# A recurrent chain and attention on one core: two buffers of L that stay, PSUM banks handed out in the order asked, and row operations written in larger pieces

## The chip, the cores and the metric

One Trainium2 chip, one of its cores. The metric is the device time of one launch in microseconds (us), the median of three runs. The core has a matrix engine (TensorE, here PE, with its weight loads as PEld), a vector engine (DVE), a scalar engine (ACT), GpSimd (POOL) and a queue that issues the transfers (SP). Each engine works through its own list of instructions in the order in which the program was written; semaphores hold one engine's instruction until another engine has done its part.

## The reference, cut to what matters

A layer of a diffusion backbone over 2048 latent tokens of width 1024 and 256 context tokens, all in fp32: a modulated norm, one input projection, then two groups of heads side by side, an output projection, a second norm and a SwiGLU network. The two groups are what the change is about:

```python
o_na = neighborhood_attention(q, k, v, kc, vc, na_rpb[l])      # 8 heads, 8 x 16 windows + all 256 context keys
o_rw, o_rwc = rwkv_bidir(feat, featc, rw_r_k[l], ...)          # 8 heads, forwards and backwards
mix = jnp.concatenate([o_na, o_rw.astype(h.dtype)], axis=-1) @ w_out[l]
...
def step(s, inp):                                              # the recurrence, token after token
    r_t, w_t, k_t, v_t, a_t, b_t = inp
    sa = jnp.einsum('bhvk,bhk->bhv', s, a_t)
    s = s * w_t[:, :, None, :] + sa[..., None] * b_t[:, :, None, :] + v_t[..., None] * k_t[:, :, None, :]
    return s, jnp.einsum('bhvk,bhk->bhv', s, r_t)
```

The recurrence starts with the 256 context tokens and goes on over the 2048 latent ones, in both directions.

## The kernel before

The program has three stages. `phase1` makes the projections and writes what both groups need to DRAM. `phase2` does the recurrence and the attention together. `phase4` does the output projection and the SwiGLU network. The change touches `phase2` and its planner `emit`, and nothing else.

**The recurrence in `phase2`** is done in blocks of 64 tokens. One *step* s (18 of them, `NS`) covers 128 tokens of each direction, so it has two *chunks* m = 2s and 2s + 1 (36 in all). Four kinds of work make it up:

- `build(s, hp, w)`: for one step and one of four pairs of heads. It loads its part of `d_b` in three transfers, asks for two PSUM banks, multiplies (L1004) and spreads the products into one of 16 units `ga`/`gb` (L1011, L1015 on DVE) and into the tile `lx` (L1010 on ACT). There are 72 of them; two streams, `builds(0)` and `builds(1)`, do two pairs of heads each. Step s uses the units `ga` numbered (4s + hp + 1) mod 16.
- `inverses()`: for each *pair* of steps (2G, 2G + 1; nine of them) the triangular 64x64 blocks in the tile `lx` of the pair are inverted in place. It begins when all eight builds of the pair are done (L1048), transposes on DVE (L1057), eliminates rows on DVE (six pairs of operations at L1070 and L1072, then seven blocks at L1078 to L1083), transposes back (L1087, L1089) and finishes with small matmuls (L1104, L1113) and copies (L1117).
- `lates(g)`: transposed operands of each chunk (L1036, L1039), one bank each.
- `chain(s, c, z, us)`: the recurrence itself, one chunk after the other: a copy of the state (L1175, L1176), matmuls L1185, L1195 and L1205 with a copy between each, two DVE operations that make the new state (L1210, L1225), the output matmuls L1218 and L1222 and their copies (L1230). Step s needs the inverse of its pair (L1151) and its four units.

`lx` holds a pair of steps: its j axis has 8 places, four for the even step and four for the odd one (`j0 = 4 * (s % 2)`). Two such buffers exist, and pair G uses buffer G mod 2. Line 976 makes a build of pair G wait until the chain has done step 2G - 3, the odd step of pair G - 2. Line 978 makes it wait for the step whose unit it takes over, s - 4.

**The attention in `phase2`** has 64 query tiles of 128. `prepare` loads and transposes operands (L670, one bank at a time), `tiles` makes scores (L740), softmax (L775 to L803 on DVE and ACT) and transposes of the probabilities (L790, L793), and `products` multiplies with v (L829) and writes each tile out (L836, L839: one L839 for a tile). Its scores live in four PSUM banks of its own.

**What sets the order.** Each of these is a Python generator that yields what it is about to do. `emit` runs nine of them side by side and writes their instructions down in the order of a plan: `("run", (engine, us))` says how long the next piece holds an engine, `("wait", ...)` and `("post", ...)` tie the streams together, and `("get", z, n)` and `("put", bank)` hand out the two PSUM banks that builds, `lates`, `prepare` and the inverses share. Before, whoever was looked at while enough banks were free got them; one that needs two could be passed by those that need one. What is written between two `run`s stays together. The plan's numbers are only used to choose an order.

Of the kernel before, what the change touches and what calls it, by code (L numbers as in the profile page):

```python
# [11 lines left out]
F32 = mybir.dt.float32  # L12
# [7 lines left out]
P = 128  # L20
# [27 lines left out]
class Run:  # L48
# [5 lines left out]
    def next(s):  # L54
        return s.k.tc.issue_after(s.last) if s.last else nullcontext()
# [806 lines left out]
def emit(banks, *streams):  # L862

    free, when = {}, {}
    banks = [(0.0, b) for b in banks]
    live = [[0.0, i, g, next(g), 0.0] for i, g in enumerate(streams)]
    while live:  # L870
        best, moved = None, False
        for e in list(live):
            while e[3] is not None and e[3][0] != "run":
                op, *args = e[3]
                if op == "post":
                    when[args[0]] = e[0]
                elif op == "put":
                    banks.extend((max(e[0], e[4]), b) for b in args)
                elif op == "get" and len(banks) >= args[1]:
                    banks.sort(key=lambda b: b[0])  # L880
                    for t, b in banks[:args[1]]:
                        e[0] = max(e[0], t)
                        args[0].append(b)
                    del banks[:args[1]]
                elif op == "wait" and all(v in when for v in args):
                    e[0] = max([e[0]] + [when[v] for v in args])
                else:
                    break
                e[3] = next(e[2], None)
                moved = True  # L890
            if e[3] is None:
                live.remove(e)
            elif e[3][0] == "run":
                key = (max(e[0], free.get(e[3][1][0], 0.0)), e[0] + LATE[e[1]], e[1])
                if best is None or key < best[0]:
                    best = (key, e)
        if best is None:
            assert moved or not live, [e[3] for e in live]
            continue
        e = best[1]  # L900
        t0 = e[0]
        for eng, us in e[3][1:]:
            t = max(t0, free.get(eng, 0.0)) if eng != "DMA" else t0
            if eng != "DMA":
                free[eng] = t + abs(us)
            e[4] = t + abs(us) + HOP
            if us > 0:
                e[0] = max(e[0], t + us + HOP)
        e[3] = next(e[2], None)


def phase2(k):
# [4 lines left out]
    with ExitStack() as ctx:  # L917
# [3 lines left out]
        lp = [ctx.enter_context(tc.tile_pool(name=f"lx{i}", bufs=1)) for i in range(2)]  # L921
# [4 lines left out]
        banks = [ps[4 + i].tile([P, 512], F32, name=f"bank{i}") for i in range(2)]  # L926
# [24 lines left out]

            return 128 * s, 128 * (1 - s if s < 2 else 19 - s)

        U, LX, ZV, TT_ = {}, {}, {}, {}

# [7 lines left out]
        def builds(w):  # L965

            for s in range(NS):
                for hp in (w, w + 2):
                    yield from build(s, hp, w)

        def build(s, hp, w):

            G, j0 = s // 2, 4 * (s % 2)
            u = units[(4 * s + hp + SHIFT) % NU]
            if G > 1:
                yield "wait", ("chain", 2 * G - 3)
            if 4 * s + hp >= NU:
                yield "wait", ("chain", (4 * s + hp - NU) // 4)
            if G not in LX:
                LX[G] = lp[G % 2].tile([P, 4, 8, 64], F32, tag="lx", name="lx")  # L980
            lx = LX[G]
            U[s, hp] = u
            src = k.d_b[hp, s]
            for h in range(2):
                if s > 1:
                    nc.sync.dma_start(out=u.ga[H[h], h:3:2 - h], in_=src[H[h], 0:512].rearrange(
                        "p (x j t) -> p x j t", x=2, j=4))
                else:
                    nc.sync.dma_start(out=u.ga[H[h], h], in_=src[H[h], 0:256].rearrange("p (j t) -> p j t", j=4))
            bk = bp.tile([P, 4, 128], F32, tag=f"bk{w}", name="bk", bufs=2)  # L990
            nc.sync.dma_start(out=bk, in_=src[:, 512:1024].rearrange("p (j t) -> p j t", j=4))
            yield "run", ("DMA", 3.0)


            N = 128 if s > 1 else 64
            z = []
            yield "get", z, 2
            yield "run", ("PE", 1.0)
            gp = [v.rearrange("p (j t) -> p j t", j=4) for v in z]
            run = Run(k)  # L1000
            for j in range(4):
                for h in range(2):
                    with run.next():
                        run.last = nc.tensor.matmul(gp[h][:, j, 0:N], bk[H[h], j], u.ga[H[h], h:3:2 - h, j, :] if s > 1  # L1004
                                                    else u.ga[H[h], h, j, :], start=True, stop=True).ins
            dc = "p (d c) t -> p d c t"
            for h in range(2):
                yield "run", ("ACT", -0.45), ("DVE", -0.34)
                ko = H[1 - h]
                nc.scalar.activation(lx[H[h], hp, j0:j0 + 4, :], gp[h][H[h], :, 0:64], AF.Copy)  # L1010
                nc.vector.tensor_tensor(u.ga[ko, h].rearrange(dc, d=2), gp[h][ko, :, 0:64].rearrange(dc, d=2),  # L1011
                                        maskS[ko, :, None, :].to_broadcast([64, 2, 2, 64]), op=ALU.mult)
                if s > 1:
                    yield "run", ("DVE", -0.34)
                    nc.vector.tensor_tensor(u.gb[:, h].rearrange(dc, d=2), gp[h][:, :, 64:128].rearrange(dc, d=2),  # L1015
                                            maskI[:, h, :, None, :].to_broadcast([P, 2, 2, 64]), op=ALU.mult)
                yield "put", z[h]
            yield "post", ("built", s, hp)
# [24 lines left out]
        def inverses():  # L1043
# [2 lines left out]

            for s in range(NS // 2):
                yield ("wait",) + tuple(("built", 2 * s + e, hp) for e in range(2) for hp in range(4))  # L1048
                lx = LX[s]
                lu = lx.rearrange("p g j t -> p (g j) t")  # L1050
                lv = lu[:, :, 0:32]
                for h in range(2):
# [11 lines left out]
                tmp = cp.tile([P, 1024], F32, tag="xT", name="xtmp")  # L1064
                for q in range(1, 4):

                    for i in range(q):
                        yield "run", ("DVE", 0.5)
                        tv = tmp[:, 0:256].rearrange("p (b t) -> p b t", b=8)
                        nc.vector.tensor_tensor(tv, xd[i][q][:, :, None].to_broadcast([P, 8, 32]), x4[:, :, q, :],  # L1070
                                                op=ALU.mult)
                        nc.vector.tensor_tensor(x4[:, :, i, :], x4[:, :, i, :], tv, op=ALU.add)  # L1072
                for q in range(4, 32, 4):

                    m, n = q, 32 - q
                    yield "run", ("DVE", 0.25 + 8 * m * n / 960)
                    tv = tmp[:, :4 * m * n].rearrange("p (c a b) -> p a c b", c=4, a=m)
                    nc.vector.tensor_tensor(tv, x[:, 0:m, q:q + 4, None].to_broadcast([P, m, 4, n]),  # L1078
                                            x[:, None, q:q + 4, q:32].to_broadcast([P, m, 4, n]), op=ALU.mult)
                    half = lambda i, k: tmp[:, i * m * n:(i + k) * m * n]  # L1080
                    nc.vector.tensor_tensor(half(0, 2), half(0, 2), half(2, 2), op=ALU.add)
                    nc.vector.tensor_tensor(half(0, 1), half(0, 1), half(1, 1), op=ALU.add)
                    nc.vector.tensor_tensor(x[:, 0:m, q:32], x[:, 0:m, q:32],  # L1083
                                            half(0, 1).rearrange("p (a b) -> p a b", a=m), op=ALU.add)
# [77 lines left out]
        dq = [(dd, q) for dd in range(2) for q in range(4)]  # L1162

        def chain(s, c, z, us):
            lx, j0 = LX[s // 2], 4 * (s % 2)
            zv = ZV[2 * s + c]
            tt = [TT_.pop((2 * s + c, g)) for g in range(2)]
            zf = z.rearrange("p d q n -> p d (q n)")
# [12 lines left out]
            run = Run(k)  # L1181
# [9 lines left out]
            run = Run(k)  # L1191
# [9 lines left out]
            run = Run(k)  # L1201
# [9 lines left out]
            if s > 1:  # L1211

                yield "run", ("PE", -1.9)
                run = Run(k)
# [23 lines left out]
        def prepare_all():  # L1238
            yield ahead
            yield from prepare  # L1240

        emit(banks, chains(), inverses(), lates(0), lates(1), builds(0), builds(1), at.products(), at.tiles(),
             prepare_all())

# [436 lines left out]
def tile_layer(tc, I):  # L1681
    with ExitStack() as ctx:
        k = K()
        setup(k, ctx, tc, I)
        setup2(k)
        phase1(k)
        with tc.tile_pool(name="mid", bufs=1) as k.mid:
            phase2(k)
            phase4(k)
# [18 lines left out]
```

## Time and profile before

| | us |
|---|---|
| median of three runs | 3523.22 (3523.1 to 3530.65) |
| the profiled execution, its own time | 3522.23 |
| its span | 3520.5 |
| `phase1`, to about | 893 |
| `phase2`, from 893 to about | 1877 |
| `phase4`, from there to the end | 3520.5 |

Over the whole span PE is busy 92% and DVE 68%. In the profile, "span" is the time from the first to the last instruction; a *window* is a stretch of it, in us from its start. For a window the profile gives the time that each engine was busy and, in brackets, the count of its instructions; `PEclk` is the granted share of TensorE's full clock (2.4 GHz), so that 0.75 is a mean over stretches at 2.4 and at 1.2 GHz. A busy PE at a lower clock does less work in the same time.

### The profile page before, as it was taken

The numbers are of one execution on the slowest core, as the hardware profiler recorded it, in microseconds if no ns is written. First come the engines' busy times: TensorE is split into PE (matmuls) and PEld (weight loads), VectorE is DVE, ScalarE is ACT, GpSimd is POOL, SyncE is SP. The second block draws the span as 40 slices with busy tenths as digits, with TensorE's granted clock in tenths as the row PEclk, the third lists the DMA queues.
The fourth block names the chain that finished last, engine by engine and source line by source line (L and its number), as shares of the span: only waits on it lengthen the run. The fifth ranks groups of instructions, "written<-read, shape, count | busy, mean of one in ns | idle before, by whom it ended". The sixth has DMA issues, their size and how long they took to land. (4 is left out here: it accounts for less than half of the span.)

```text
span 3520.5 us, 66352 instructions
## 1 busy us (share of the span) xinstructions
PE 3239.0 (92%) x25202; PEld 2775.8 (79%) x25202; DVE 2396.8 (68%) x4489; ACT 1465.8 (42%) x3186; POOL 1101.2 (31%) x1057
## 2 busy tenths in 40 slices
PE   7899999999879889798856999999899999999999
PEld 5787878789657677576655887888799998899998
DVE  7758786774385766847655754444877778777776
ACT  4524343442445556465433553233333334333332
POOL 3425543453000100100113433333433334433332
PEclk9999999999888899899877999999999999999999
DMA  7546666553634446354326554332422223422222
GB/s 244 160 140 198 189 193 199 160 172 113 194 105 130 142 126 196 97 166 126 87 78 189 183 174 159 96 102 84 150 63 72 67 72 102 135 72 72 66 64 69
DMA packets 461856, 458.50 MB, mean 130 GB/s; under 512 B 56656, under 2 KB 381664, under 8 KB 461536
## 3 DMA queue, kind: packets, MB, share of 16 engines
q1 hardware_dynamic: 461536, 454.25, 42.7%
q8 instruction: 199, 3.26, 0.4%
q14 instruction: 121, 0.99, 0.1%
HBM read 346.37 MB, written 107.75 MB: 129 GB/s over the span
## 5 line engine op out<-in xcount | busy, mean ns | idle before, releaser
L1329 ACT ACTIVATE w<-raw 128x512 fp32r<-128x512 f32 x440 | 270.9, 627 | 497.8 <-PE acc L1618 190.2
L1538 PE MATMUL acc<-ua,w 128*128 128x384 f32 x2464 | 469.8, 336 | 6.0 <-POOL w L1330 2.7
L1618 PE MATMUL acc<-w,fh 128*128 128x512 f32 x1408 | 435.7, 394 | 18.7 <-ACT fh L1329 7.3
L1330 DVE TENSOR_TENSOR w<-raw,w 128x512 fp32r<-128x512 f32 x308 | 273.3, 891 | 247.0 <-ACT w L1329 120.0
L1538 PEld LDWEIGHTS acc<-ua,w 128*128 128x128 f32 x2464 | 433.2, 189 | 9.9 <-POOL w L1330 4.2
L219 PE MATMUL acc<-u,wh 128*128 128x512 f32 (+3 forms) x1120 | 347.9, 390 | 11.4 <-DVE sh L257 6.7
L1618 PEld LDWEIGHTS acc<-w,fh 128*128 128x128 f32 x1408 | 266.4, 190 | 79.4 <-ACT fh L1329 9.1
L503 PE MATMUL acc<-wt,u 128*128 128x256 f32 x2496 | 321.1, 287 | 5.0 <-DVE sh L257 2.3
L503 PEld LDWEIGHTS acc<-wt,u 128*128 128x128 f32 x2496 | 307.9, 194 | 12.3 <-issue 4.6
L1609 POOL TENSOR_TENSOR raw<-raw,gate 128x512 f32<-128x512 f32 x132 | 179.3, 1369 | 409.8 <-DMA raw<-in_w_dram 354.1
L1330 POOL TENSOR_TENSOR w<-raw,w 128x512 fp32r<-128x512 f32 x132 | 186.2, 1411 | 272.0 <-PE acc L1538 57.6
L1618 PE MATMUL acc<-w,fl 128*128 128x512 f32 x704 | 269.4, 392 | 0.1
L1538 PE MATMUL acc<-ux,w 128*128 128x384 f32 x1232 | 252.1, 335 | 0.3 <-DVE w L1330 0.3
L219 PEld LDWEIGHTS acc<-u,wh 128*128 128x128 f32 (+1 forms) x1120 | 206.0, 191 | 58.5 <-issue 7.0
L1520 PE MATMUL acc<-ua,w 128*128 128x512 f32 x1056 | 241.7, 389 | 2.0 <-POOL w L1330 1.1
L1520 PEld LDWEIGHTS acc<-ua,w 128*128 128x128 f32 x1056 | 198.0, 188 | 43.7 <-POOL w L1330 1.6
L219 PE MATMUL acc<-u,wl 128*128 128x512 f32 (+3 forms) x560 | 218.0, 389 | 2.8 <-DVE wl L210 2.7
L1538 PEld LDWEIGHTS acc<-ux,w 128*128 128x128 f32 x1232 | 216.8, 188 | 1.6 <-DVE w L1330 1.0
L1623 DVE TENSOR_TENSOR h<-h,acc 128x512 f32<-128x512 f32 x192 | 126.3, 683 | 100.3 <-PE acc L1618 100.1
L1179 POOL COPY zp<-z 64x512 f32<-64x512 f32 x64 | 41.4, 647 | 453.4 <-PE up L1218 293.7
L1330 POOL TENSOR_TENSOR w<-s,w 128x512 fp32r<-128x512 f32 x88 | 131.6, 1496 | 152.5 <-PE acc L1538 56.6
L1530 DVE TENSOR_TENSOR t<-acc,t 128x384 f32<-128x384 f32 x308 | 169.7, 551 | 13.9 <-PE acc L1538 7.3
(256 smaller groups left out, 6728.9 us busy)
## 6 DMA issues: line engine op xcount, KB each, us to landing
raw<-in_w_dram SPq DMA_DIRECT2D x132, 512.0 KB
raw<-in_w_dram SPq DMA_DIRECT2D x132, 256.0 KB
wada<-in_w_ada_dram SPq DMA_DIRECT2D x96, 256.0 KB
d_b<-bk SPq DMA_DIRECT2D x72, 256.0 KB
bkl<-d_b SPq DMA_DIRECT2D x144, 128.0 KB
bk<-d_b SPq DMA_DIRECT2D x72, 256.0 KB
d_b<-ar SPq DMA_DIRECT2D x136, 128.0 KB
xt<-in_x_dram SPq DMA_DIRECT2D x32, 512.0 KB
```

The source lines that it names most:

```text
L219: nc.tensor.matmul(acc[:m, :n], a_[:, kk % 4, :m], b_[b][:, kk, :], start=(i == 0), stop=(i == 23))
L503: nc.tensor.matmul(acc[:, 256 * e:256 * e + 256], a_[b][:, kk, (j + e) * P:(j + e + 1) * P], ws[kk][:, h, :], start=(i == 0), stop=(i == 23))
L1179: nc.gpsimd.tensor_copy(zp[H[h], h], z[H[h]])
L1329: nc.scalar.activation(hl[0], v, AF.Copy)
L1330: eng.tensor_tensor(hl[1], v, hl[0].bitcast(F32), op=sub)
L1520: nc.tensor.matmul(acc, hl[wi][:, kk, :], u[ui][:, 4 * hf + kk, :], start=q == 0, stop=q == 23)
L1530: vadd = lambda o, x, y: nc.vector.tensor_tensor(o, x, y, op=add)
L1538: nc.tensor.matmul(acc, w[wi][:, kk, :], u[i][ui][:, kk, :], start=q == 0, stop=q == 11)
L1609: nc.gpsimd.tensor_tensor(raw, raw, g2[:, o], op=ALU.mult)
L1618: nc.tensor.matmul(acc, a_[:, f, ts], w2[f][:, hl, :], start=(i == 0), stop=(i == 6 * np_ - 1))
L1623: nc.vector.tensor_tensor(hs[j][:, o], hs[j][:, o], acc, op=add)
```

## The change

Three edits, which change no instruction and no count, only the order:

- `LX` becomes two tiles that are made once; a build of step s waits for the chain's step s - 4, which used the same half of the same buffer, and no longer for the odd step of that pair. For odd s this is the step that it waited for before. For even s it is one step earlier: step 8 waits for step 4, where it waited for step 5.
- `emit` keeps a list `asked`: banks go to the stream that asked first, and the others wait behind it, whatever they need.
- In `inverses()` the row operations are announced to the planner in six runs and no longer in thirteen: the six pairs of L1070 and L1072 in two runs of three pairs, the seven blocks of L1078 to L1083 in four runs of two blocks (the last has one). The time announced for the six pairs is 5.2 us, and was 3.0 us.

```diff
--- before.py
+++ after.py
@@ -864,7 +864,8 @@
 
 
 
-    free, when = {}, {}
+
+    free, when, asked = {}, {}, []
     banks = [(0.0, b) for b in banks]
     live = [[0.0, i, g, next(g), 0.0] for i, g in enumerate(streams)]
     while live:
@@ -876,7 +877,11 @@
                     when[args[0]] = e[0]
                 elif op == "put":
                     banks.extend((max(e[0], e[4]), b) for b in args)
-                elif op == "get" and len(banks) >= args[1]:
+                elif op == "get" and e not in asked:
+                    asked.append(e)
+                    continue
+                elif op == "get" and asked[0] is e and len(banks) >= args[1]:
+                    asked.pop(0)
                     banks.sort(key=lambda b: b[0])
                     for t, b in banks[:args[1]]:
                         e[0] = max(e[0], t)
@@ -951,7 +956,9 @@
 
             return 128 * s, 128 * (1 - s if s < 2 else 19 - s)
 
-        U, LX, ZV, TT_ = {}, {}, {}, {}
+        U, ZV, TT_ = {}, {}, {}
+
+        LX = [lp[i].tile([P, 4, 8, 64], F32, name=f"lx{i}") for i in range(2)]
 
 
 
@@ -972,13 +979,11 @@
 
             G, j0 = s // 2, 4 * (s % 2)
             u = units[(4 * s + hp + SHIFT) % NU]
-            if G > 1:
-                yield "wait", ("chain", 2 * G - 3)
+            if s > 3:
+                yield "wait", ("chain", s - 4)
             if 4 * s + hp >= NU:
                 yield "wait", ("chain", (4 * s + hp - NU) // 4)
-            if G not in LX:
-                LX[G] = lp[G % 2].tile([P, 4, 8, 64], F32, tag="lx", name="lx")
-            lx = LX[G]
+            lx = LX[G % 2]
             U[s, hp] = u
             src = k.d_b[hp, s]
             for h in range(2):
@@ -1046,7 +1051,7 @@
 
             for s in range(NS // 2):
                 yield ("wait",) + tuple(("built", 2 * s + e, hp) for e in range(2) for hp in range(4))
-                lx = LX[s]
+                lx = LX[s % 2]
                 lu = lx.rearrange("p g j t -> p (g j) t")
                 lv = lu[:, :, 0:32]
                 for h in range(2):
@@ -1064,8 +1069,9 @@
                 tmp = cp.tile([P, 1024], F32, tag="xT", name="xtmp")
                 for q in range(1, 4):
 
+                    if q % 2:
+                        yield "run", ("DVE", 1.0 if q == 1 else 4.2)
                     for i in range(q):
-                        yield "run", ("DVE", 0.5)
                         tv = tmp[:, 0:256].rearrange("p (b t) -> p b t", b=8)
                         nc.vector.tensor_tensor(tv, xd[i][q][:, :, None].to_broadcast([P, 8, 32]), x4[:, :, q, :],
                                                 op=ALU.mult)
@@ -1073,7 +1079,8 @@
                 for q in range(4, 32, 4):
 
                     m, n = q, 32 - q
-                    yield "run", ("DVE", 0.25 + 8 * m * n / 960)
+                    if q % 8 == 4:
+                        yield "run", ("DVE", sum(0.25 + 8 * r * (32 - r) / 960 for r in (q, q + 4) if r < 32))
                     tv = tmp[:, :4 * m * n].rearrange("p (c a b) -> p a c b", c=4, a=m)
                     nc.vector.tensor_tensor(tv, x[:, 0:m, q:q + 4, None].to_broadcast([P, m, 4, n]),
                                             x[:, None, q:q + 4, q:32].to_broadcast([P, m, 4, n]), op=ALU.mult)
@@ -1162,7 +1169,7 @@
         dq = [(dd, q) for dd in range(2) for q in range(4)]
 
         def chain(s, c, z, us):
-            lx, j0 = LX[s // 2], 4 * (s % 2)
+            lx, j0 = LX[s // 2 % 2], 4 * (s % 2)
             zv = ZV[2 * s + c]
             tt = [TT_.pop((2 * s + c, g)) for g in range(2)]
             zf = z.rearrange("p d q n -> p d (q n)")
```

How the order of the instructions moves, at three places. Lines behind the first edit are 1 to 7 higher in the changed kernel (L1004 becomes L1009, L1185 becomes L1192, L1210 and L1225 become L1217 and L1232, L1078 to L1083 become L1085 to L1090).

PE, before, at the first build of step 8: `ga9` to `ga12` are the units of step 6, and `ga1` is the first unit of step 8.

```order
L1185 MATMUL rp_9726<-zv_13970,ga9_9762 64x64 x2
L1185 MATMUL rp_9726<-zv_13970,ga10_9764 64x64 x2
L1185 MATMUL rp_9726<-zv_13970,ga11_9766 64x64 x2
L1185 MATMUL rp_9726<-zv_13970,ga12_9768 64x64 x2
L1004 MATMUL bank1_9725<-ga1_9746,bk_14276 128x128
L1004 MATMUL bank0_9724<-ga1_9746,bk_14276 128x128
```

PE, after, at the same build: `ga5` to `ga8` are the units of step 5.

```order
L1192 MATMUL rp_9726<-zv_12958,ga5_9756 64x64 x2
L1192 MATMUL rp_9726<-zv_12958,ga6_9758 64x64 x2
L1192 MATMUL rp_9726<-zv_12958,ga7_9760 64x64 x2
L1192 MATMUL rp_9726<-zv_12958,ga8_9762 64x64 x2
L1009 MATMUL bank1_9725<-ga1_9748,bk_13171 128x128
L1009 MATMUL bank0_9724<-ga1_9748,bk_13171 128x128
```

The builds of step 8 stood behind the first products of step 6 and stand now behind the first products of step 5.

DVE, before, in the blocks of the inverse of steps 8 and 9 (`xtmp_15452` and `lu_15420`). Between its first and last instruction there is none of the chain's (L1176, L1199, L1210, L1225); here L1011 and L1015 belong to builds, L776, L839 and L775 to the attention.

```order
L1078 TENSOR_TENSOR xtmp_15452<-lu_15420 128x12x4x20
L1011 TENSOR_TENSOR ga12_9768<-bank1_9725,maskS_9729 64x256
L1015 TENSOR_TENSOR gb12_9769<-bank1_9725,maskI_9728 128x256
L1011 TENSOR_TENSOR ga12_9768<-bank0_9724,maskS_9729 64x256
L1015 TENSOR_TENSOR gb12_9769<-bank0_9724,maskI_9728 128x256
L1081 TENSOR_TENSOR xtmp_15452<-xtmp_15452 128x480
L776 ISA pr_15582,st_15581<-sw0_9778,es_15253 128x512
L776 ISA st_15581 128x1
L1082 TENSOR_TENSOR xtmp_15452<-xtmp_15452 128x240
L839 TENSOR_TENSOR ot_15602<-sx1_9781,st_15434 128x128
L775 TENSOR_REDUCE st_15581<-sx1_9781 128x1
```

DVE, after, in the same inverse (`xtmp_14231` and `lu_14207`): L1217, L1232 and L1183 belong to the chain, L802, L775 and L803 to the attention.

```order
L1217 TENSOR_TENSOR z2_14458<-rp_9726,z2_14233 128x512
L1088 TENSOR_TENSOR xtmp_14231<-xtmp_14231 128x480
L1232 TENSOR_TENSOR z2_14458<-z2_14458,pc_79 128x512
L1089 TENSOR_TENSOR xtmp_14231<-xtmp_14231 128x240
L802 TENSOR_TENSOR st_14611<-st_14611 128x2
L775 TENSOR_REDUCE st_14797<-sx0_9782 128x1
L1183 COPY zv_14289<-z2_14458 64x512
L1090 TENSOR_TENSOR lu_14207<-lu_14207,xtmp_14231 128x12x20
L803 RECIPROCAL st_14611<-st_14611 128x2
L1085 TENSOR_TENSOR xtmp_14231<-lu_14207 128x16x4x16
```

The inverse of steps 8 and 9 stood alone between two steps of the chain, and now three chunks of the chain (of steps 6 and 7) stand in among its rows. The pieces that are announced as one are not unbroken in the program either before or after.

PE, before, at the end of `phase2`: the last output matmuls of the chain (L1218, L1222), then the first ones of `phase4` (L1416, L1458, L1279). The last L836 of the attention stands some 300 rows ahead of them.

```order
L1218 MATMUL up_9727<-zp_9776,ga7_9758 64x64 x2
L1222 MATMUL up_9727<-zv_20533,gb7_9759 64x64 x2
L1218 MATMUL up_9727<-zp_9776,ga8_9760 64x64 x2
L1222 MATMUL up_9727<-zv_20533,gb8_9761 64x64 x2
L1416 MATMUL mtp_20960<-ident_62,mx_20904 128x128 x4
L1458 MATMUL acc_21020<-wo0_20857,mh_20958 128x512 x2
L1458 MATMUL acc_21047<-wo0_20857,mh_20958 128x512 x2
```

PE, after, at the end of `phase2`: the last tiles of the attention (L793, L790, L829, L836), with a first transpose of `phase4` (L1423) among them.

```order
L793 MATMUL sw0_9780<-ident_62,pr_20678 128x128 x3
L790 MATMUL sx1_9783<-ident_62,pr_20678 128x128 x2
L793 MATMUL sw1_9781<-ident_62,pr_20678 128x128 x3
L790 MATMUL sx0_9782<-ident_62,pr_20678 128x128 x2
L1423 MATMUL mtp_20953<-ident_62,mx_20897 128x128 x4
L836 MATMUL sx1_9783<-ident_62,oT_20709 128x128
L829 MATMUL sx0_9782<-pr_20678,vw_20719 64x128 x6
L829 MATMUL sx0_9782<-pr_20678,vc_17830 64x128 x4
L836 MATMUL sx1_9783<-ident_62,oT_20733 128x128
L1286 MATMUL g_20906<-gup_20802,gd_20901 128x512
L1465 MATMUL acc_21013<-wo0_20850,mh_20951 128x512
```

The chain was what `phase2` ended with, and now it is the attention: four of its 64 tiles (by L836) stand behind the chain's last output matmul. The first tile of `mx`, the input of `phase4`, is loaded and transposed ahead of that end; the splits of `w_out` (L1329, L1330 on ACT and DVE), which stood among the chain's last chunks, now stand behind the last attention tile on both engines.

## Rows read from the trace of the kernel before

**Rows 1.** Busy time by window: PE, PEld, DVE, ACT, POOL, PEclk, DMA share, GB/s

```profile
893.00:1753.00 860.00, 732.84 (x10499) 578.73 (x10500) 569.51 (x1462) 469.01 (x1258) 76.45 (x92) 0.88 0.49 137
1753.00:1877.00 124.00, 71.72 (x1630) 64.49 (x1628) 66.92 (x115) 44.02 (x77) 14.08 (x19) 0.77 0.38 109
1877.00:1913.00 36.00, 22.88 (x81) 16.54 (x82) 20.47 (x30) 6.64 (x10) 18.48 (x14) 0.76 0.70 225
```

**Rows 2.** L1225 alone (the chain's last state operation) by window: DVE, PEclk, DMA

```profile
1753.00:1877.00 124.00, 5.54 (x8) 0.77 0.38 109
...
1290.00:1390.00 100.00, 3.43 (x5) 1.00 0.66 182
...
1490.00:1600.00 110.00, 4.13 (x6) 0.97 0.58 165
```

**Rows 3.** L839 alone (the attention's last operation of a tile) by window

```profile
1290.00:1390.00 100.00, 2.59 (x9) 1.00 0.66 182
...
1490.00:1600.00 110.00, 2.60 (x9) 0.97 0.58 165
```

**Rows 4.** Busy time by window, as in the first group, inside the run

```profile
1290.00:1390.00 100.00, 96.38 (x1547) 78.90 (x1539) 52.96 (x165) 67.62 (x189) 6.77 (x12) 1.00 0.66 182
1390.00:1490.00 100.00, 77.09 (x999) 60.49 (x997) 86.47 (x205) 47.45 (x125) 11.88 (x12) 0.85 0.37 110
1490.00:1600.00 110.00, 102.70 (x1769) 84.23 (x1770) 57.34 (x162) 70.44 (x188) 9.36 (x14) 0.97 0.58 165
```

**Rows 5.** Timeline of DVE around steps 4 to 8: start, us, instruction

```profile
1270.88 0.69 DVE L1225 TENSOR_TENSOR z<-z,pc 128x512 f32<-128x512 f32 x1
...
1303.42 0.68 DVE L1225 TENSOR_TENSOR z<-z,pc 128x512 f32<-128x512 f32 x1
...
1370.97 0.69 DVE L1225 TENSOR_TENSOR z<-z,pc 128x512 f32<-128x512 f32 x1
...
1397.07 2.12 DVE L1057 STREAM_TRANSPOSE lu<-lx 128x1024 f32<-128x1024 f32 x1
...
1455.02 0.69 DVE L1117 COPY lx<-bank 32x512 f32<-32x512 f32 x1
...
1471.36 0.68 DVE L1225 TENSOR_TENSOR z<-z,pc 128x512 f32<-128x512 f32 x1
```

**Rows 6.** Timeline of PE after step 5: the first build of step 8

```profile
1310.44 1.04 PE L1004 MATMUL bank<-ga,bk 64*128 64x128 f32 x13
```

**Rows 7.** Busy time by window: the inverses of steps 8, 9 and 10, 11

```profile
1397.00:1456.00 59.00, 43.95 (x533) 33.50 (x532) 48.70 (x114) 26.37 (x70) 6.10 (x6) 0.80 0.28 84
...
1453.00:1508.00 55.00, 45.18 (x901) 37.28 (x897) 45.31 (x96) 28.93 (x70) 7.83 (x9) 0.94 0.38 107
```

**Rows 8.** Groups by line: the blocks of an inverse; busy, mean ns, idle before

```profile
L1078 DVE TENSOR_TENSOR xtmp<-lu 128x448 f32<-128x448 f32 (+3 forms) x63 | 60.2, 955 | 1.3
...
L1081 DVE TENSOR_TENSOR xtmp<-xtmp 128x224 f32<-128x224 f32 (+3 forms) x63 | 35.9, 571 | 1.3
...
L1083 DVE TENSOR_TENSOR lu<-lu,xtmp 128x112 f32<-128x112 f32 (+3 forms) x63 | 22.6, 359 | 1.0
...
L1082 DVE TENSOR_TENSOR xtmp<-xtmp 128x112 f32<-128x112 f32 (+3 forms) x63 | 22.3, 354 | 1.2
```

**Rows 9.** Timelines of SP, ACT, PE and DVE where `phase4` begins

```profile
1850.45 3.21 SPq L1395 DMA_DIRECT2D raw<-in_w_out_dram  x5
...
1855.13 1.06 ACT L1329 ACTIVATE wo<-raw 128x1024 fp32r<-128x1024 f32 x1 [1.18 <-DMA raw<-in_w_out_dram]
...
1857.84 1.06 ACT L1329 ACTIVATE wo<-raw 128x1024 fp32r<-128x1024 f32 x1 [1.66 <-DMA raw<-in_w_out_dram]
...
1886.91 1.08 PE L1416 MATMUL mtp<-ident,mx 128*128 128x128 f32 x4 [11.45 <-DMA mx<-d_mix]
...
1909.93 0.68 DVE L1465 TENSOR_TENSOR h<-acc,gate 128x512 f32<-128x512 f32 x1
```

## The prediction

> **What bounds the kernel now.** I read the busy time by window first. The change reaches only the stretch from 893 to 1877 us, in which recurrence and attention run together, and that stretch has two parts [rows 1]. Up to 1753 us, where the last attention tile is written, PE is busy 732.84 us at a granted 0.88 of its full clock: 732.84 x 0.88 = 645 us of work at full clock in 860 us, 0.750 per us. DVE is busy 66% and ACT 55%; nothing is full on the mean. From 1753 to 1877 us the chain is alone, with the last eight of its 36 chunks [rows 2] and the ninth inverse: 71.72 x 0.77 = 55 us of PE work in 124 us, 0.45 per us. The reader is to see that this tail has no partner.
>
> Smaller windows show why the first part is not full: two regimes take turns [rows 4]. In the 100 us from 1290 and the 110 us from 1490 no inverse runs; PE is at (96.38 + 102.70 x 0.97) / 210 = 0.933 per us and DVE only half busy, and 18 tiles [rows 3] and 11 chunks [rows 2] get done. In the 100 us from 1390 an inverse is always running: DVE is 86% busy and PE falls to 77% at a clock of 0.85.
>
> The timeline says what alternates. The chain ends step 4 at 1271.6 us and step 5 at 1304.1 us, and the first build of step 8, which waits for step 5, starts at 1310.4 [rows 5, 6]. The eight builds of the pair last until the inverse of steps 8 and 9 starts at 1397.1; it ends at 1455.7. Step 7 ended at 1371.7, so for 84 us the chain had nothing to do, and then the next inverse ran beside it. The first of these two inverses (no chain beside it) has PE at 43.95 x 0.80 / 59 = 0.596 per us, the second (chain beside it) at 45.18 x 0.94 / 55 = 0.772 [rows 7].
>
> **The change part by part.** No instruction is added or removed, so the cost is in what stands beside what. The sum is made against the profiled execution's 3522.2 us; the median of the runs is 1 us longer, and I count them as the same.
>
> *The tail is shared.* By the order at the end of this stage the attention now ends behind the chain, so the 55 us of PE work move into a run with attention beside them. At the rate of the first part they take 55.2 / 0.750 = 74 us in place of 124: -50. If they only ran as fast as an inverse without the chain they would take 93: -31. At 0.933 they would take 59: -65. I take -50, because the ninth inverse comes along, which rules out the best rate, while seven eighths of the tail's chunks are ordinary ones.
>
> *Even steps build one step earlier.* Step 8 may start at 1271.6 and not at 1304.1: 32.5 us. By the order the inverse of steps 8 and 9 then lies beside three chunks, and before beside none. While 32.5 us of such a stall turn into a stretch with the chain in it, PE gains 32.5 x (0.772 - 0.596) / 0.750 = 7.6 us. There are three such places (steps 4, 8 and 12; the fourth, step 16, lies in the tail): -23. The bound from below is nothing, if the inverses still end as late; from above 3 x 32.5 x (0.933 - 0.596) / 0.750 = -44. With each build its three transfers move forward in SP's queue; DMA is 49% busy there [rows 1], and I charge nothing.
>
> *Banks in the order asked.* It changes how long eight builds take: 1310.4 to about 1397 for one pair. A build that needs two banks is no longer passed by those that need one, but it also holds these up. What that does to an inverse's start is at most of the size of the term above, with either sign (+-19); I take 0 since the trace has no row for a bank that is waited for.
>
> *Larger pieces.* The instructions are the same, so DVE's busy time is too; a block costs 955 + 571 + 354 + 359 = 2240 ns [rows 8], and two that are announced together 4.5 us. I take 0: what hides it is that other operations still stand between the rows of a piece, as the order of DVE shows. If that cover were gone, see the slower rival.
>
> *A new end.* Four tiles stand behind the chain's last matmul. No row shows attention without the chain. With the chain beside it a tile takes 210 / 18 = 11.7 us without inverses and 860 / 64 = 13.4 us on the mean, so four are 47 to 54 us. Taking at most 55.2 / 8 = 6.9 us of PE work for a chunk, a tile has (0.933 x 210 - 11 x 6.9) / 18 = 6.7, four 27, worth 36 us at 0.750. Cost 11 to 18, or 0 if they run as fast as the mix; the nearest row is the one without inverses: +11.
>
> *The start of the next stage.* Before, the first result there comes at 1909.9, 33 us after the chain, with an 11.45 us wait for `mx` [rows 9]. That wait goes, since `mx` is loaded earlier. What is late next is `w_out`: its splits now stand behind the last tile, and the last four of its eight pieces load only when the first four are split. A load took 1850.45 to 1855.13 until its split, the next 2.7 us more, so the last is split some 1 + 4.7 + 3 x 2.7 + 1 = 15 us after the attention's end. The first result could come after 17 us (-16), or the splits, on ACT and DVE beside the last tile's remains, could add 10. I take half of the wait that goes: -6.
>
> Sum: 3522.2 - 50 - 23 + 11 - 6 = 3454 us.
>
> **The rivals.**
>
> *Only the tail is shared, and at the worst rate.* The inverses run one after another on DVE, and each now has more chunks and tiles among its rows, so it may end as late as before. For it: DVE at 86% in such a stretch [rows 4]. Then the 55 us cost 93 and the second term is lost: 3522.2 - 31 + 11 - 6 = 3496.
>
> *The attention is late by as much as the chain is early.* If a tile waits for each chunk and inverse that is put before it, the attention takes 124 us longer and the sum is only the new end and start: 3522.2 + 11 - 6 = 3527. For it: 13.4 us a tile in the mix against 11.7 without inverses. Against it: PE at 0.750 where 0.933 is shown.
>
> *Slower: one queue on DVE ties chain and inverse together.* In the new order the chain's state operations stand between the rows of the inverse, so each of them waits for the block ahead of it, and everything behind waits when the chain's matmuls are late. With pieces of two blocks the mean wait grows by half of 2.24 us, 1.1 us. 27 chunks (three beside each inverse) with four DVE operations give 108 x 1.1 = 119 us if each meets a piece, and 32 us if they meet it by chance (seven blocks are 15.7 of some 58 us, 27%). At the middle, 75: 3522.2 - 50 + 11 - 6 + 75 = 3552. It decides from 45 / 108 = 0.4 us per operation on, provided that the chain still sets the pace. Against it: the chain is idle for 84 us in each such period now, and this slack is spent first. The Trainium skill speaks for this rival: Perfetto Trace Analysis, section Optimizing Scalar/DVE Operations, says that where Vector is not saturated but makes other engines idle, breaking work into smaller pieces may let it finish sooner. DVE is such an engine here on the mean (66%), yet not in the stretches of the inverses (82 to 86%), where the larger pieces are.
>
> **How the numbers follow.** Forecast 0.66, tail only 0.13, late attention 0.11, slower 0.10. Less than 0.3% (10.6 us) this measurement cannot tell from no change. The forecast and the first rival are faster: 0.78, leaving 0.01 of the forecast's spread; the second is the same: 0.12; the last is slower: 0.10. The forecast's own range is 3405 (-65, -44, 0 and -16, with half of the banks' term against it) to 3485 (-31, 0, +11, -6 and half of the banks' term as a gain). The range for 8 in 10 goes on to 3527, which takes in both middle rivals and leaves out the slower one.
>
> **What would show it.** Right: the last L839 of the attention (same line after) comes at about 1877 - 62 = 1815 us, some 50 us behind the chain's last state operation (L1232 after); the window from 893 to there has PE near 0.78 to 0.8 per us, and windows of 100 us in it no longer alternate between 0.65 and 0.95; the first L1016 of step 8 comes during step 5; the first result of the next stage is some 25 to 30 us behind the last tile. Wrong: gaps of the chain of 80 us that stay (the first rival); tiles of 15 us (the second); DVE over 85% busy while PE waits for L1217, L1232 or L1206 (the third).

## The result, and the profile after

The changed kernel takes 3465.33 us (median, 3461.15 to 3467.26) against 3524.22 us of the kernel before on the same chip: ratio 0.9827, 95% interval [0.9812, 0.9843]. Its profiled execution took 3461.15 us with a span of 3459.4, 61 us less than before; forecast were 68 less.

Of these 61 us, 57 are the end of `phase2`, which came from 1875.1 us (the chain) to 1818.5 us (the attention), and 4 are what follows it (1645.4 and 1641.0 us to the end of the span). The busy time by window shows the same stretch as before (columns as in [rows 1]): while both streams run, what stands behind the chain, and the start of `phase4`.

```profile
893.00:1792.00 899.00, 780.10 (x11918) 620.44 (x11917) 624.71 (x1536) 494.74 (x1285) 92.99 (x111) 0.90 0.50 142
1792.00:1818.00 26.00, 17.51 (x199) 13.03 (x200) 11.80 (x40) 14.12 (x45) 7.18 (x6) 0.92 0.67 217
1818.00:1852.00 34.00, 26.31 (x103) 18.84 (x103) 27.54 (x37) 11.04 (x14) 13.02 (x10) 0.86 0.70 197
```

The lone chain of 124 us at a clock of 0.77 is gone. In its place there are 26 us of lone attention at 0.92. Over the whole stretch PE gives (780.10 x 0.90 + 17.51 x 0.92) / 925 = 0.776 per us; before it was (645 + 55) / 984 = 0.711.

Windows of 100 us inside the run, which answer to [rows 4], and ahead of them the start of `phase2`:

```profile
893.00:1000.00 107.00, 85.65 (x804) 66.41 (x804) 62.67 (x159) 43.51 (x121) 8.70 (x9) 0.71 0.51 148
...
1100.00:1200.00 100.00, 83.40 (x1348) 66.85 (x1346) 73.74 (x182) 56.86 (x149) 13.61 (x16) 0.97 0.55 154
1200.00:1300.00 100.00, 86.03 (x1481) 68.77 (x1483) 74.22 (x177) 57.96 (x145) 12.21 (x15) 0.98 0.54 153
1300.00:1400.00 100.00, 88.36 (x1388) 72.07 (x1384) 74.74 (x186) 56.43 (x149) 11.35 (x13) 0.91 0.51 142
1400.00:1500.00 100.00, 89.20 (x1511) 71.97 (x1511) 78.32 (x192) 57.34 (x151) 10.65 (x13) 0.97 0.56 161
1500.00:1600.00 100.00, 89.34 (x1400) 71.76 (x1402) 71.40 (x173) 59.77 (x151) 13.40 (x15) 0.90 0.54 149
```

From 1100 to 1600 us the two regimes are gone: PE is at 0.80 to 0.87 per us in each window (in [rows 4] 0.66 to 0.96), DVE at 71 to 78% (there 52 to 86). The start is not as even: in the first 107 us PE gives 85.65 x 0.71 / 107 = 0.57 per us.

DVE around steps 4 to 8 answers to [rows 5] (start, us, instruction): L1232 ends a chunk of the chain, L1016 belongs to the builds, L1062 opens the inverse of steps 8 and 9, and L1124 is near its end.

```profile
1204.42 0.67 DVE L1232 TENSOR_TENSOR z<-z,pc 128x512 f32<-128x512 f32 x1
1211.77 0.43 DVE L1016 TENSOR_TENSOR ga<-bank,maskS 64x256 f32<-64x256 f32 x1 [0.96 <-ACT lx L1015]
...
1235.90 0.68 DVE L1232 TENSOR_TENSOR z<-z,pc 128x512 f32<-128x512 f32 x1
...
1291.62 2.18 DVE L1062 STREAM_TRANSPOSE lu<-lx 128x1024 f32<-128x1024 f32 x1
1293.69 0.64 DVE L1232 TENSOR_TENSOR z<-z,pc 128x512 f32<-128x512 f32 x1
1313.80 0.68 DVE L1232 TENSOR_TENSOR z<-z,pc 128x512 f32<-128x512 f32 x1
1331.52 0.68 DVE L1232 TENSOR_TENSOR z<-z,pc 128x512 f32<-128x512 f32 x1
1363.74 0.69 DVE L1124 COPY lx<-bank 32x512 f32<-32x512 f32 x1 [0.25 <-ACT lx L1124]
1375.93 0.67 DVE L1232 TENSOR_TENSOR z<-z,pc 128x512 f32<-128x512 f32 x1
```

Step 4 ends at 1205.1 and step 8 is built from 1211.8 on, while step 5 runs to 1236.6. Three chunks end beside the inverse. From the end of step 7 (1332.2) to that of the next chunk (1376.6) it is 44 us; before it was 1371.7 to 1472.0, 100 us.

The two inverses of [rows 7], by window:

```profile
1291.00:1365.00 74.00, 63.58 (x1043) 51.22 (x1038) 59.50 (x140) 45.10 (x120) 7.51 (x9) 0.94 0.55 157
1380.00:1453.00 73.00, 64.25 (x1099) 50.91 (x1100) 54.58 (x134) 41.98 (x110) 7.38 (x9) 0.93 0.55 152
```

An inverse takes longer, 73 us where it took 55 to 59, but PE runs at 0.81 and 0.82 beside it where it had 0.60 and 0.77. DVE is at 80 and 75% and no longer at 82.

DVE at the end of `phase2`: L839 ends a tile, and the first L1472 is the first result of `phase4` ([rows 9] before).

```profile
1791.49 0.68 DVE L1232 TENSOR_TENSOR z<-z,pc 128x512 f32<-128x512 f32 x1
1797.08 0.29 DVE L839 TENSOR_TENSOR ot<-sx,st 128x128 f32<-128x128 f32 x1 [0.86 <-PE sx L790]
1804.85 0.29 DVE L839 TENSOR_TENSOR ot<-sx,st 128x128 f32<-128x128 f32 x1 [1.36 <-ACT pr L796]
1816.59 0.28 DVE L839 TENSOR_TENSOR ot<-sx,st 128x128 f32<-128x128 f32 x1
1818.16 0.29 DVE L839 TENSOR_TENSOR ot<-sx,st 128x128 f32<-128x128 f32 x1 [0.63 <-PE sx L836]
1847.52 0.68 DVE L1472 TENSOR_TENSOR h<-acc,gate 128x512 f32<-128x512 f32 x1
```

And ACT there, with the splits of `w_out`:

```profile
1817.49 3.89 ACT L1336 ACTIVATE wo<-raw 128x1024 fp32r<-128x1024 f32 x4
1826.39 1.06 ACT L1336 ACTIVATE wo<-raw 128x1024 fp32r<-128x1024 f32 x1 [4.49 <-DMA raw<-in_w_out_dram]
...
1833.15 1.06 ACT L1336 ACTIVATE wo<-raw 128x1024 fp32r<-128x1024 f32 x1 [1.21 <-DMA raw<-in_w_out_dram]
```

Four splits start as soon as ACT has done its part of the last tile, and four wait for loads that the first four let go. The last is done 16 us behind the attention (15 were estimated), and the first result comes 29 us behind it.

### The profile page after: what moved, and what is told of

Read it like the earlier page. It is cut to its first block, busy times and chain, and to the rows that moved or that the text cites. A ratio compares the mean times of both kernels' runs of the same rounds, so it can differ in the third digit from the quotient of the medians.

```text
span 3459.4 us, 66443 instructions
## 1 busy us (share of the span) xinstructions
PE 3233.9 (93%) x25202; PEld 2764.8 (80%) x25202; DVE 2405.0 (70%) x4489; ACT 1464.9 (42%) x3186; POOL 1109.4 (32%) x1057
## 5 line engine op out<-in xcount | busy, mean ns | idle before, releaser
L1337 DVE TENSOR_TENSOR w<-raw,w 128x512 fp32r<-128x512 f32 x308 | 284.1, 926 | 247.6 <-ACT w L1336 123.2
```

What stands on the lines that cost most here:

```text
L1337: eng.tensor_tensor(hl[1], v, hl[0].bitcast(F32), op=sub)
```

## Experiments

Each ratio is to the kernel before, timed on the same chip in the same batch; microseconds that are made from a ratio are taken of 3524 us.

**e1_late0: all three edits, but the attention is not held back** in the planner's ranking, so that the tail comes back. Two theories: the gain is the shared tail, or it is the inverses that spread over the run.

```
-LATE = (0, 0, -10, -10, 0, 0, 0, 60, 0)
+LATE = (0, 0, -10, -10, 0, 0, 0, 0, 0)
```

> All three edits, but the planner's delay for the attention's tiles is 0 and not 60, so the attention is written earlier: by the order nine chunks and two inverses stand behind its last tile again (eight chunks and one in the kernel before). Sharing the tail is the gain: the 50 us come back, and the time is 3500 to 3530. Earlier builds and spread inverses are the gain, wherever the tail is: they are all still there, and the time is 3455 to 3475.

Measured: 3496.18 us, 0.9913 [0.9883, 0.9943]. The attention ends at 1713.0 us and the chain at 1842.1:

```profile
893.00:1713.00 820.00, 742.04 (x10208) 568.14 (x10206) 566.96 (x1459) 463.84 (x1247) 77.00 (x90) 0.92 0.50 142
1713.00:1842.00 129.00, 96.95 (x1936) 85.30 (x1929) 72.50 (x118) 49.87 (x86) 17.17 (x21) 0.75 0.42 116
```

With a tail as long as before, nine chunks in 129 us, 31 us of the gain remain (0.0087 x 3524), and some 30 us are lost. Neither theory alone is right. That the 30 us are the tail is not shown by this run alone: the attention is earlier in the whole stage, and from the end of its first chunk to that of its last the chain takes 820 us here and 780 in the changed kernel.

**e2_no_lx, e3_no_fifo, e4_no_big: the changed kernel with one edit undone** (the hunks are shortened to the lines that matter).

```
 e2  -            if s > 3:
     -                yield "wait", ("chain", s - 4)
     +            if G > 1:
     +                yield "wait", ("chain", 2 * G - 3)
     ...                                                            # and LX by pair again
 e3  -                elif op == "get" and asked[0] is e and len(banks) >= args[1]:
     +                elif op == "get" and len(banks) >= args[1]:
 e4  +                        yield "run", ("DVE", 0.5)               # ahead of every pair again
     +                    yield "run", ("DVE", 0.25 + 8 * m * n / 960)  # ahead of every block again
```

> The changed kernel without the two buffers that stay: a build waits for the odd step of its buffer's last pair, as before. Banks in order and larger pieces are kept. By the order five chunks and one inverse stand behind the last tile. Sharing the tail: five of eight chunks and the inverse are unshared, so about a third of the 50 us is won and no new end is paid: 3500 to 3512. If the earlier build by itself is the gain, nothing is left: 3520. If banks or pieces are the gain: 3465.

> The changed kernel without the banks in the order asked. By the order four chunks and one inverse stand behind the last tile. Sharing the tail: 3495 to 3510. If the two buffers and the earlier build are the gain: 3470 or less. If the bank queue is the gain alone: 3520.

> The changed kernel with the row operations in thirteen runs as before. By the order the attention still ends last, with six tiles behind the last chunk (four in the changed kernel). Sharing the tail: as the changed kernel with two more tiles at its end, 3465 to 3475. If the larger pieces delay the chain on the vector engine (the slower rival), this one is faster than the changed kernel by 10 us or more: 3455 or less. If larger pieces are what gains, it is at 3500.

Measured: e2 3513.19 us, 0.9941 [0.9923, 0.9959]; e3 3494.73 us, 0.9894 [0.9867, 0.9920]; e4 3474.01 us, 0.9827 [0.9797, 0.9857]. On top of the others the earlier wait is worth 40 us (0.9941 - 0.9827), the banks 24, and the larger pieces nothing that is measurable. In e2 and e3 a tail of 81 and 57 us is back, in e4 none: its chain ends at 1795.9 and its attention at 1836.9.

**e5_lx, e6_fifo, e7_big: the kernel before with one edit alone** (the same hunks the other way round).

> The kernel before with the two buffers that stay alone (even steps may build one step earlier). By the order five chunks and one inverse stand behind the last tile (eight and one before). If the parts simply add, this is what leaving it out cost: 40 us in the earlier run, so 3485 or a ratio of 0.988. Sharing the tail: three of eight chunks are shared, a third of 50 us with little of the spread, so 10 to 25 us, a ratio of 0.993 to 0.997.

> The kernel before with the banks in the order asked alone. By the order four chunks and one inverse stand behind the last tile. If the parts add, 24 us, a ratio of 0.993. Sharing the tail: half of it is shared, 15 to 30 us, a ratio of 0.991 to 0.996. If the queue only helps builds that may start early, nothing: 1.000.

> The kernel before with the larger pieces alone. By the order four chunks and one inverse stand behind the last tile. If pieces neither cost nor gain by themselves, as on top of the other two edits, but a shorter tail is what counts: 15 to 30 us, a ratio of 0.991 to 0.996. If the parts add: 1.000, since leaving them out cost nothing. If they cost on the vector engine: over 1.000.

Measured: e5 3484.21 us, 0.9877 [0.9843, 0.9911]; e6 3499.88 us, 0.9919 [0.99, 0.9939]; e7 3518.46 us, 0.9966 [0.9952, 0.9979]. Alone they are worth 43, 29 and 12 us, together 84; the change as a whole gave 61. So the gains overlap. e5 is where adding the parts put it (0.988) and outside what a shared tail alone would have given it (0.993 to 0.997). For e5 the same windows and the gap behind step 7:

```profile
893.00:1745.00 852.00, 750.77 (x11079) 596.82 (x11078) 589.17 (x1503) 484.70 (x1291) 81.61 (x101) 0.90 0.51 143
1745.00:1831.00 86.00, 42.99 (x1042) 38.43 (x1041) 47.71 (x74) 26.99 (x43) 8.86 (x11) 0.70 0.39 108
```

```profile
1355.63 0.69 DVE L1225 TENSOR_TENSOR z<-z,pc 128x512 f32<-128x512 f32 x1
...
1432.29 0.69 DVE L1225 TENSOR_TENSOR z<-z,pc 128x512 f32<-128x512 f32 x1
```

This gap is 77 us where it was 100; the two others of its kind went from 99 and 97 to 76 and 75. The chain ends at 1831.2, 44 us earlier. Of 68 us of shorter gaps nearly two thirds arrive at its end.

**e9_lx_oldwait: LX made once, but with the old wait.** Only the wait differs from e5, so it tells the tile that is made once from the earlier build.

> The kernel before with the two buffers made once, but a build still waits for the odd step of its buffer's last pair. If the earlier build is what the buffers' edit gained (43 us alone), nothing is left here: a ratio of 0.997 to 1.003. If the buffer that is not handed out anew gains by itself: 0.988 to 0.995.

Measured: 3529.5 us, 1.0004 [0.9989, 1.002]; the gaps are 98, 18, 99, 19, 97 us again. Of this edit only the wait counts.

**e12_times: the kernel before with a truer time announced** for a pair of row operations (0.87 us; its own trace gives 421 + 421 ns, that of the changed kernel 452 + 438). It moves no piece together.

```
-                        yield "run", ("DVE", 0.5)
+                        yield "run", ("DVE", 0.87)
```

> The kernel before with the six row operations still announced one by one, but at the 0.87 us that they take and not at 0.5 us; pieces, buffers and banks as before. By the order nine chunks and two inverses stand behind the last tile (eight and one before). If the larger pieces alone gained 12 us because the plan knew their true time, this one gains as much: 0.996. If they gained by the tail (four chunks), this one does not: 1.000 to 1.006.

Measured: 3508.06 us, 0.9947 [0.9926, 0.9967].

```profile
893.00:1690.00 797.00, 698.53 (x10020) 550.22 (x10020) 538.32 (x1407) 459.66 (x1239) 71.81 (x88) 0.91 0.52 145
1690.00:1862.00 172.00, 96.71 (x2130) 86.98 (x2126) 98.70 (x169) 53.61 (x95) 18.08 (x24) 0.70 0.34 95
```

The attention ends at 1689.9 us and the chain at 1861.6: a tail of 172 us, 50 longer than before, and yet 19 us faster. The chain's gaps behind steps 3, 5, 7, 9 and 11 are 69, 44, 40, 57 and 39 us; before they were 99, 18, 100, 20 and 97. So a long tail alone does not tell a slow stage, and what e7 gained alone may be its truer time (5.2 us in place of 3.0) as much as its larger pieces; these two were not parted.

**e8_wp: the changed kernel with the tiles of `w_out` in the place in SBUF that the chain has left**, so that their splits need not wait for the attention (six of the eight now stand ahead of its end).

```
-                w = wp[KD - 1 - kk].tile([P, 2, D], F32R, name=f"wo{kk}")
+                w = wp[kk].tile([P, 2, D], F32R, name=f"wo{kk}")      # and wp's pools opened behind mq5
```

> The changed kernel with the eight tiles of w_out moved in SBUF, from the place of the attention's buffers to the place of the recurrence's, which come free first. By the order six of the eight splits on the scalar and vector engines now stand ahead of the attention's end (none in the changed kernel). If the start of the next stage waits for w_out, the 29 us from the last tile to its first result become 15 to 20 and the time falls by 8 to 14 us, to a ratio of about 0.979. If that start is bound by the time-mix output of the first two tiles, it is unchanged: 0.983.

Measured: 3474.85 us, 0.9845 [0.9824, 0.9867], no gain on 0.9827. DVE at the end of `phase2`:

```profile
1797.18 0.28 DVE L839 TENSOR_TENSOR ot<-sx,st 128x128 f32<-128x128 f32 x1
1804.49 0.29 DVE L839 TENSOR_TENSOR ot<-sx,st 128x128 f32<-128x128 f32 x1 [0.63 <-PE sx L790]
1820.23 0.28 DVE L839 TENSOR_TENSOR ot<-sx,st 128x128 f32<-128x128 f32 x1
1830.70 0.29 DVE L839 TENSOR_TENSOR ot<-sx,st 128x128 f32<-128x128 f32 x1 [0.35 <-ACT pr L796]
1834.89 0.29 DVE L839 TENSOR_TENSOR ot<-sx,st 128x128 f32<-128x128 f32 x1 [3.90 <-PE sx L836]
1855.13 0.69 DVE L1472 TENSOR_TENSOR h<-acc,gate 128x512 f32<-128x512 f32 x1
```

The first result comes 20 us behind the attention and no longer 29. But the last two tiles are 14 and 17 us later, since work of `phase4` now stands ahead of theirs on ACT and DVE. What the next stage won, the end of this one paid; which of the two explanations expected above is right stays open.

**e10_late15, e11_late10: the changed kernel with the attention held back less** (15 and 10 in the same place of `LATE`), so that both streams might end at once.

> All three edits, with 15 in place of 60 as the planner's delay of the attention's tiles. By the order chain and attention end together (one tile behind the last chunk; four in the changed kernel, nine chunks behind the last tile with 0). If the shared tail is worth the 28 us between those two, this one keeps them and saves some of the attention's lone end: a ratio of 0.980 to 0.984. If the gain of the changed kernel over the one with 0 comes from the attention being held back throughout, it lies between them, 0.985 to 0.989.

> The same with 10: by the order one chunk stands behind the last tile. Sharing the tail: all but one chunk of some 10 us is shared, 0.981 to 0.985. If the attention's place throughout counts: 0.986 to 0.990.

Measured: 3475.41 us, 0.9855 [0.9831, 0.9878], and 3467.07 us, 0.9832 [0.9807, 0.9856]. With 15 chain and attention end at 1804.8 and 1807.4, with 10 at 1811.1 and 1799.1, and the first result comes at 1850.5 and 1849.1 (1847.5 in the changed kernel). With e4, whose attention ends 41 us behind its chain, these intervals all meet that of the changed kernel: once the ends are that close, which one is last is not told by the time. Of the two theories, e11 lies where sharing the tail put it (0.981 to 0.985), and e10's interval takes in both; so 10 in `LATE`, which leaves a tail of 12 us, brings what 60 brings, and that speaks for the tail in e1's 30 us without proving it. No version beat the changed kernel.

## Why the prediction came out

The direction, the end of the attention (1818 us; 1815 were named), the even windows, the builds of step 8 during step 5 and the first result 29 us behind the last tile came as said. One sign did not: the attention ends 27 us behind the chain's last state operation, and 50 were named. Term by term it looks less good.

*The shared tail and the new end* were sized -50 and +11, together -39. e1 against the changed kernel gives about -30 for both, with the attention's other place in it. The -50 was too large by its own rule: 71.72 x 0.77 = 55 is a product of two means, and summed over windows of 2 us the tail has 61 us of PE work, which at 0.750 take 81, so -43. The new end cost less: four tiles in 26 us, not 47 to 54. At 0.776 per us their 17.51 x 0.92 = 16 us of PE work would have taken 21, so it cost 5 us. These are 6.6 us of time for a tile where the row without inverses that I chose gave 11.7, and 4.0 us of PE work where I had 6.7; part of their work stands ahead of the chain's end (18 of the 32 score matmuls L740 of four tiles lie in this window).

*Even steps one step earlier* were sized -23, with -44 as the bound. The runs give -43 alone (e5) and -40 on top of the other edits. The mechanism is as said, the size is not: I priced a gap by the PE rate that comes back, 7.6 us each. But in the kernel before the chain ended last, and most of what such a chain's gaps lose arrives at its end: in e5 three times 23 us, and 44 of them at the end.

*Banks* were taken as 0, with 19 either way. They gave -29 alone, which is outside the bound, and -24 on top of the others, whose interval reaches into it. I had looked at one pair in the middle; what moves is the start of `phase2`. These are the first and last start of the chain's last state operation (36 chunks) and of the transpose that opens an inverse (nine), in the kernel before, the changed kernel, e6 and e3, then the transpose before and in e6:

```profile
L1225 DVE TENSOR_TENSOR z<-z,pc x36: 670/691/694, 1039.8 to 1874.4; 128x512 f32<-128x512 f32 x36
L1232 DVE TENSOR_TENSOR z<-z,pc x36: 644/684/694, 1011.8 to 1791.5; 128x512 f32<-128x512 f32 x36
L1229 DVE TENSOR_TENSOR z<-z,pc x36: 671/691/699, 1010.1 to 1853.1; 128x512 f32<-128x512 f32 x36
L1227 DVE TENSOR_TENSOR z<-z,pc x36: 673/686/694, 1053.4 to 1847.6; 128x512 f32<-128x512 f32 x36
...
L1057 DVE STREAM_TRANSPOSE lu<-lx x9: 2104/2131/2186, 971.2 to 1790.4; 128x1024 f32<-128x1024 f32 x9
L1061 DVE STREAM_TRANSPOSE lu<-lx x9: 2126/2156/2201, 933.1 to 1762.7; 128x1024 f32<-128x1024 f32 x9
```

With the banks in the order asked the first inverse starts 38 us earlier (971 to 933 us) and the first chunk comes 30 us earlier; from first to last chunk e6 then takes 843 us, and before 835. So the gain of e6 lies at the start and not in its gaps of 62, 37, 89, 19, 87 us. In all eight runs with this edit the first chunk ends at 1009 to 1022 us, in the six without it at 1040 to 1054. Who had been passed is seen in the matmuls from 893 to 935 us, of the builds (L1004, L1008 in e6) and of `prepare` (L670), before and in e6:

```profile
893.00:935.00 42.00, 8.16 (x78) 7.40 (x78) 0.76 0.83 220
893.00:935.00 42.00, 21.95 (x144) 19.57 (x144) 0.55 0.76 215
...
893.00:935.00 42.00, 5.68 (x24) 3.70 (x24) 0.76 0.83 220
893.00:935.00 42.00, 3.61 (x12) 2.01 (x12) 0.55 0.76 215
```

The builds, which need two banks, were held up by `prepare`, which needs one: 78 matmuls of builds beside 24 of `prepare` became 144 beside 12.

*Larger pieces* were taken as 0, and are 0 on top of the rest (e4). The blocks take what they took: 966 + 557 + 371 + 370 = 2264 ns against 2240 in [rows 8], from these groups by line, of DVE from 893 to 1818 us in the changed kernel:

```profile
L1085 DVE TENSOR_TENSOR xtmp<-lu 128x448 f32<-128x448 f32 (+3 forms) x63 | 60.9, 966 | 0.9
...
L1088 DVE TENSOR_TENSOR xtmp<-xtmp 128x224 f32<-128x224 f32 (+3 forms) x63 | 35.1, 557 | 0.9
...
L1089 DVE TENSOR_TENSOR xtmp<-xtmp 128x112 f32<-128x112 f32 (+3 forms) x63 | 23.4, 371 | 0.8
L1090 DVE TENSOR_TENSOR lu<-lu,xtmp 128x112 f32<-128x112 f32 (+3 forms) x63 | 23.3, 370 | 1.3
```

*The next stage's start*, -6, came as -4 by the time from there to the end. By the first result it is the same -6: 29 us behind the last tile against 35 behind the chain's last state operation (1909.9 - 1875.1; the 33 of the prediction count from 1877).

So the total, 68 us forecast and 61 measured, held in part by luck: two terms were too small (banks, earlier builds) and one too large (the tail), and the edits overlap: e5, e6 and e7 each shortened the tail too, from 122 to 86, 64 and 80 us, which the others would have shared. I had added the terms as if they were independent.

One step was weak: PE's busy time times its clock was treated as a fixed amount of work. By the products it was 700 us before and is 718 now with the same instructions; half of this is the product of means in the tail, since by windows of 2 us it is 709 and 718. A rate of 718 / 925 = 0.776 against 709 / 984 = 0.721, 8% more, shortened the stretch by 6%.

*The rivals.* "Only the tail" fell with e1, which keeps 31 us of the gain with a tail that is not shared; the gaps of 80 us that were its sign are 43 to 51 in the changed kernel. "Late attention" came half true: 60 tiles in 899 us are 15.0 us each and the attention ends 65 us later, not 124. The sign that I named for it, tiles of 15 us, was badly chosen, since my own end at 1815 us means 14.4. "Slower" fell with the result, 61 us faster where it had 30 us slower, and with e4, which without the larger pieces is no faster. The Trainium skill (Perfetto Trace Analysis, Optimizing Scalar/DVE Operations), which I had called on for this rival, speaks of breaking up instructions where they make other engines idle. No instruction is split or joined here, so no run tests its sentence; what the runs show is that smaller planned pieces finish no sooner, 0.9827 either way, and that PE is 86 to 88% busy in the windows of those inverses.

## What to carry over

When two streams share the engines, look at which of them ends last and whether the run alternates between regimes; both are seen in windows of 100 us. Price a gap in the stream that ends last nearer to its own length than to the engine time that it leaves idle: 44 of 68 us arrived here, in one run (e5). Look at the start of that stream too: all that the banks gained alone lay ahead of its first chunk. Test the edits of a planner one by one from both sides: here the three were worth 84 us alone and 61 together, and one of them nothing on top of the others.

## What was not expected

- The same inverse takes 38 us without company (the last one of the kernel before), 54 to 60 in partial company, and 58 to 81 with chain and attention beside it; yet the stage is shorter by 57 us, so the length of an inverse alone does not tell what it costs.
- The granted clock of a lone chain is 0.69 to 0.77 in all nine runs where it is alone for 57 us or more (0.77 before, 0.75 in e1, 0.71 in e2, 0.73 in e3, 0.70 in e5, 0.69 in e6, 0.70 in e7, 0.76 in e9, 0.70 in e12), between the two levels of 1.2 and 2.4 GHz, while PE is busy 48 to 75% there; before that, beside the attention, it is 0.87 to 0.92. The tail loses twice: PE waits, and what it does is slower.
- A lone attention does not always keep the clock: it had 0.92 in the changed kernel's 26 us, 0.80 in e4's 41 us and 0.68 in e8's 38 us.
